# Input projections of a hybrid encoder in one core: pairs of units as seven block products, tokens in three parts

## Chip, core and metric

The kernel runs on one core of a Trainium2 chip. The core has a matmul engine (TensorE, PE), a vector engine (VectorE, DVE), an activation engine (ScalarE, ACT), a general engine (GpSimd, POOL) and a queue engine (SyncE, SP) that issues nearly all transfers; sixteen DMA engines move the data. The metric is the device time of one execution in microseconds (us), the median of several runs.

## What is computed

One step of an encoder layer with two attention branches, over 2,176 tokens (2,048 of a prompt, 128 of running streams) of width 1,024. Cut to the part that the change touches:

```
h    = rms_norm(x, g_in)                        # (2176, 1024)
proj = einsum('btd,de->bte', h, w_in)           # w_in: 1024 x 4928
qa, ka, va, z_a, qd, ckv_in, kpe_in, z_b, m_a, m_b = split(proj)
qa, ka = rope(qa, pos), rope(ka, pos)           # 512 columns each
# va: 512; z_a, z_b: 512 each, used as silu(z); qd: 512; ckv_in: 256; kpe_in: 64
# m_a, m_b: 1024 each, merge gates
```

Then come the latent projections, differential and latent attention, the gates, the output projections, the residual and a last normalisation. Everything is float32 outside. Inside, each factor of a large product is split into a rounded high part and a remainder (`hi`, `lo`, type float32r), and a product is three matmuls: hi x hi, hi x lo, lo x hi (`_mm3`, L94 to L101).

## The kernel before

`build` runs `_phase_a` (the input projections but for the merge gates), `_phase_a2` (latent projections), `_phase_b` (attention of the prompt), `_gates` (merge gates, groups of tokens that fill holes of the other stages), `_sample` (running streams) and `_phase_c` (output). Instructions are ordered by a list scheduler that simulates the engines: among those that are ready it takes the one with the highest priority, which is the program's order, except where code asks for another (`ahead()` in `_gates` asks for the priority that follows `_phase_a`). Tiles come from pools with a fixed number of buffers; a tile waits until the readers of the buffer's last tile are done.

In `_phase_a` the tokens stand transposed (`xT`, features on partitions), in six groups `GROUPS` of 384 columns (the last 256). `load_group` keeps the high and low parts of all groups in SBUF (`hi0` to `hi5`, `lo0` to `lo5`), scaled by the gain `g_in` but not by the tokens' root mean square. Squares are summed by GpSimd and VectorE, `stats` adds them over partitions with small matmuls and spreads 1/rms over R; R multiplies the results as they leave PSUM (L232, L233, L254, L260).

A unit is 128 columns of `w_in` (8 blocks of 128 features). For each group it takes 8 x 3 = 24 matmuls into one PSUM bank (`unit_psum`). 22 units are taken here: 4 for `qd`, 2 for `ckv_in`, 8 for rotary queries and keys (pairs, `rope_block`), 8 for the gates z (L260 to L263). `first_units` takes the first two as the groups arrive. Values run with tokens as the stationary operand, two passes of 256 columns (`v_block`); the rotary key of the latent branch has 16 matmuls a group (`kpe_block`). Between blocks, 16 further units for the merge gates are split and written to DRAM (`wz`), to be read by `_gates`.

Staging tiles for raw weights and tokens come from `c.zs` (2 buffers) and a pool of 1; split weights from `c.zw` (4) and a pool of 2; results from a pool of 6 and `c.zt` (4). `c.zh` holds group 0's tokens here, and later the tokens of `_gates`. Each split is a ScalarE copy (L112) and a VectorE subtraction (L113).

Of the kernel before, what the change touches and what calls it, by code (L numbers as in the profile page):

```python
# [38 lines left out]


# [4 lines left out]
def _consts(c, pool):  # L45
# [14 lines left out]
    c.rstd = pool.tile([P, NT], F32, name="rstd")  # L60
# [66 lines left out]
def _phase_a(c):  # L127
    nc, tc = c.nc, c.tc
    with (
        tc.tile_pool(name="a_h", bufs=1) as ph,  # L130
        tc.tile_pool(name="a_w", bufs=2) as pw,
        tc.tile_pool(name="a_s", bufs=1) as pst,
        tc.tile_pool(name="a_t", bufs=6) as pt,
# [3 lines left out]
        hi, lo, sums = [], [], []  # L137
        R = pc.tile([P, T], F32, name="R")
        count = {"st": 0, "w": 0, "t": 0}

        def stage(shape, name):
            count["st"] += 1
            return (pst if count["st"] % 3 == 0 else c.zs).tile(shape, F32, tag="st", name=name)

        def tmp(n, name, m=P):
            return pt.tile([P, NG], F32, tag="t", name=name)[:m, :n]

        def tmp2(n, name, m=P):
            return c.zt.tile([P, NG], F32, tag="t", name=name)[:m, :n]

        def load_group(g):
            t0, n = GROUPS[g]
            pool = c.zh if g < 1 else ph
            a = pool.tile([P, KT, n], F32R, tag=f"hi{g}", name=f"hi{g}")
            b = pool.tile([P, KT, n], F32R, tag=f"lo{g}", name=f"lo{g}")
            hi.append(a)
            lo.append(b)
            for k2 in range(4):
                if k2 % 2:
                    st = pc.tile([P, 2, NG], F32, tag="cs", name=f"xt{g}_{k2}", bufs=2)  # L160
                else:
                    st = stage([P, 2, NG], f"xt{g}_{k2}")
                nc.sync.dma_start(st[:, :, :n], c.i["xT"][:, 2 * k2 : 2 * k2 + 2, t0 : t0 + n])
                for k in range(2):
                    kt = 2 * k2 + k
                    gain = c.g_in[:, kt : kt + 1]
                    if k:
                        nc.gpsimd.tensor_scalar(a[:, kt, :], st[:, k, :n], gain, 1.0, op0=ALU.mult, op1=ALU.mult)
                    else:
                        nc.scalar.activation(a[:, kt, :], st[:, k, :n], AF.Copy, scale=gain)  # L170
                    nc.vector.scalar_tensor_tensor(
                        b[:, kt, :], st[:, k, :n], gain, a[:, kt, :].bitcast(F32), op0=ALU.mult, op1=ALU.subtract
                    )
                for k in range(2):
                    if k2 + k == 0:
                        total = pc.tile([P, NG], F32, tag="sq", name=f"sq{g}", bufs=2)[:, :n]
                        nc.scalar.square(total, st[:, k, :n])
                    else:
                        sq = tmp(n, f"sq{g}_{k2}_{k}")
                        nc.scalar.square(sq, st[:, k, :n])  # L180
                        (nc.gpsimd if k else nc.vector).tensor_tensor(total, total, sq, op=ALU.add)
            sums.append(total)

        def stats(g):
            t0, n = GROUPS[g]
            ta, tb = t0 // P, (t0 + n) // P
            ps = pp.tile([P, 512], F32, tag="ps", name=f"pss{g}")
            for t in range(tb - ta):
                nc.tensor.matmul(ps[:, t : t + 1], sums[g][:, t * P : (t + 1) * P], c.ones[:, 0:1], start=True, stop=True)
            nc.vector.tensor_copy(c.rstd[:, ta:tb], ps[:, : tb - ta])  # L190
            _rsqrt(c, c.rstd[:, ta:tb], c.rstd[:, ta:tb], 1.0 / D)
            yield
            ps = pp.tile([P, 512], F32, tag="ps", name=f"psr{g}")
            for t in range(ta, tb):
                dg = tmp(P, f"dg{t}")
                nc.vector.tensor_scalar(dg, c.ident, c.rstd[:, t : t + 1], None, op0=ALU.mult)
                nc.tensor.matmul(ps[:, (t - ta) * P : (t - ta + 1) * P], c.ones, dg, start=True, stop=True)
            nc.scalar.copy(R[:, t0 : t0 + n], ps[:, :n])
            nc.sync.dma_start(c.Rh[:, t0 : t0 + n], R[:, t0 : t0 + n])

        def weights(src, name):
            k, n = src.shape[1], src.shape[2]
            st = stage([P, k, n], f"ws_{name}")
            nc.sync.dma_start(st, src)
            count["w"] += 1
            pool = pw if count["w"] % 3 == 0 else c.zw
            a = pool.tile([P, k, n], F32R, tag="w", name=f"wh_{name}")
            b = pool.tile([P, k, n], F32R, tag="w", name=f"wl_{name}")
            _split(nc, a, b, st)
            return a, b  # L210

        def unit_psum(w, g, name, m=P):
            n = GROUPS[g][1]
            ps = pp.tile([P, 512], F32, tag="ps", name=f"ps_{name}_{g}")
            _mm3(
                nc, ps[:m, :n],
                [(w[0][:, kt, :], w[1][:, kt, :], hi[g][:, kt, :], lo[g][:, kt, :]) for kt in range(KT)],
            )
            return ps[:m, :n]

        def rope_block(u0, dst, pair, out, scale):
            ws = [weights(c.i["wu"][u0 + i], f"u{u0 + i}") for i in range(2)]
            for g, (t0, n) in enumerate(GROUPS):
                nm = f"r{u0}_{g}"
                pa = unit_psum(ws[0], g, f"u{u0}")
                pb = unit_psum(ws[1], g, f"u{u0 + 1}")
                cs = pc.tile([P, 2, NG], F32, tag="cs", name=f"cs{nm}", bufs=2)
                nc.sync.dma_start(cs[:, :, :n], c.i["rope"][:, :, t0 : t0 + n])
                co, si = cs[:, 0, :n], cs[:, 1, :n]
                Rg = R[:, t0 : t0 + n]  # L230
                ta, tb = tmp(n, f"ta{nm}"), tmp(n, f"tb{nm}")
                nc.vector.tensor_tensor(ta, pa, Rg, op=ALU.mult)  # L232
                nc.vector.tensor_tensor(tb, pb, Rg, op=ALU.mult)  # L233
# [7 lines left out]
                for half, (r, x, y) in enumerate(((m1, ta, m2), (m3, tb, m4))):  # L241
                    if out is not None:
                        nc.sync.dma_start(out[pair, half, :, t0 : t0 + n], r)
                    xr, yr = x.bitcast(F32R), y.bitcast(F32R)
                    nc.scalar.mul(xr, r, scale)
                    nc.vector.scalar_tensor_tensor(yr, r, scale, x, op0=ALU.mult, op1=ALU.subtract)
                    for hl, z in enumerate((x, y)):
                        nc.sync.dma_start(dst[pair, hl, half, :, t0 : t0 + n], z)
# [16 lines left out]
        def units(us):  # L265
            ws = [weights(src, nm) for src, nm, _ in us]
            for g in range(len(GROUPS)):
                for w, (src, nm, ev) in zip(ws, us):
                    ev(unit_psum(w, g, nm), g)
# [1116 lines left out]
```

## Time and profile before

| | |
|---|---|
| median of 3 runs | 2661.29 us (2658.8 to 2663.44) |
| profiled execution, its time | 2662.93 us |
| profiled execution, its span | 2661.1 us, 44,909 instructions |
| PE busy | 2513.8 us, 94% |
| DVE busy | 1442.7 us, 54% |
| ACT busy | 1066.6 us, 40% |
| POOL busy | 704.2 us, 26% |
| DMA | 496.17 MB, mean 186 GB/s |

Busy time is a union: two matmuls in flight count once, so the durations of single matmuls add up to more. The page also shows the granted clock of TensorE in tenths of 2.4 GHz; a timeline row gives the start, the duration, the engine, the line of the kernel, the operation with its output and inputs, and in brackets how long the engine sat idle before it and what ended that.

### The profile page before, as it was taken

What the parts mean: (1) busy time and instruction counts of PE and PEld (TensorE: products, weight loads), DVE (VectorE), ACT (ScalarE), POOL (GpSimd) and SP (SyncE); (2) the same over time, 40 slices, a digit from 0 to 9 for tenths busy, and PEclk for the clock granted to TensorE, in tenths of its full rate; (3) what the DMA queues carried; (4) which work ended last, traced back from release to release, by engine and by line L of the source; (5) the groups of instructions that cost most, each with busy time, mean ns of one, the idle gap of its engine ahead of it and who ended that gap; (6) DMA issues with size and microseconds to landing.
All of it is one profiled execution on the core that took longest, in us unless ns stands there. A gap on an engine that the chain in (4) does not pass through costs nothing. (4 is left out here: it accounts for less than half of the span.)

```text
span 2661.1 us, 44909 instructions
## 1 busy us (share of the span) xinstructions
PE 2513.8 (94%) x16308; PEld 2254.8 (85%) x16308; DVE 1442.7 (54%) x3038; ACT 1066.6 (40%) x2682; POOL 704.2 (26%) x946
## 2 busy tenths in 40 slices
PE   7999999999897989999999999998999997999998
PEld 7999899999787879998988898887676774888887
DVE  8236662233565657877785577896333323433333
ACT  5101213212333356766675566775334333311111
POOL 7102220001333333334343333544101001122221
PEclk9999999999898999999999999999999998999999
DMA  5346777422667893365566657523887676534332
GB/s 182 120 150 200 253 255 234 143 69 83 183 228 228 259 280 108 123 179 157 171 183 200 210 175 230 155 77 125 342 326 302 253 299 212 179 125 131 127 112 93
DMA packets 291372, 496.17 MB, mean 186 GB/s; under 512 B 27440, under 2 KB 229200, under 8 KB 280144
## 3 DMA queue, kind: packets, MB, share of 16 engines
q1 hardware_dynamic: 291152, 493.31, 56.3%
q8 instruction: 129, 2.11, 0.3%
q14 instruction: 91, 0.75, 0.1%
HBM read 351.55 MB, written 141.66 MB: 185 GB/s over the span
## 5 line engine op out<-in xcount | busy, mean ns | idle before, releaser
L98 PE MATMUL z<-z_hi,zw 128*128 128x384 f32 (+1 forms) x768 | 263.2, 343 | 26.2 <-ACT zt L388 22.1
L100 PE MATMUL z<-z_hi,zw 128*128 128x384 f32 (+1 forms) x768 | 257.2, 335 | 2.3 <-DMA zw<-wz 2.3
L99 PE MATMUL z<-z_lo,zw 128*128 128x384 f32 (+1 forms) x768 | 258.0, 336 | 0.6 <-POOL z_lo L370 0.6
L990 DVE TENSOR_REDUCE pmd<-sd 128x1 f32<-128x512 f32 (+3 forms) x320 | 189.4, 603 | 55.6 <-PE sd L1091 27.8
L992 ACT ACTIVATE ed<-sd,pmd 128x512 f32<-128x512 f32 (+3 forms) x320 | 200.4, 630 | 46.6 <-DVE pmd L990 32.8
L1091 PE MATMUL sd<-k,q 128*128 128x512 f32 (+2 forms) x640 | 189.9, 384 | 2.6 <-ACT ed L992 1.5
L1031 POOL TENSOR_SCALAR ed<-ed,ad 128x512 f32<-128x512 f32 (+3 forms) x160 | 116.2, 741 | 282.4 <-DVE ad L1007 129.3
L98 PEld LDWEIGHTS z<-z_hi,zw 128*128 128x128 f32 x768 | 148.2, 193 | 45.5 <-ACT zt L388 28.2
L99 PEld LDWEIGHTS z<-z_lo,zw 128*128 128x128 f32 x768 | 148.2, 193 | 8.9 <-issue 6.3
L100 PEld LDWEIGHTS z<-z_hi,zw 128*128 128x128 f32 x768 | 147.8, 192 | 8.2 <-issue 3.7
L1031 POOL TENSOR_SCALAR em<-em,am 128x512 f32<-128x512 f32 (+3 forms) x160 | 104.0, 665 | 152.3 <-DVE am L1007 93.0
L113 DVE TENSOR_TENSOR zw<-zs,zw 128x512 fp32r<-128x512 f32 x128 | 91.0, 737 | 86.2 <-ACT zw L112 85.9
L370 POOL TENSOR_TENSOR z_lo<-zx,z_hi 128x384 fp32r<-128x384 f32 (+1 forms) x48 | 48.3, 1032 | 333.0 <-DVE gt L260 262.7
L98 PE MATMUL y<-o,wh_ab 128*128 128x384 f32 (+1 forms) x384 | 127.8, 333 | 8.5 <-DVE sm L1212 8.5
L98 PE MATMUL ps_u<-hi,wh_u 128*128 128x384 f32 (+1 forms) x384 | 126.6, 330 | 7.5 <-ACT wh_u L112 7.5
L100 PE MATMUL y<-o,wl_ab 128*128 128x384 f32 (+1 forms) x384 | 126.7, 330 | 0.6 <-DVE wl_ab L113 0.6
L99 PE MATMUL y<-o,wh_ab 128*128 128x384 f32 (+1 forms) x384 | 126.8, 330 | 0.0
L99 PE MATMUL ps_u<-lo,wh_u 128*128 128x384 f32 (+1 forms) x384 | 126.2, 329 | 0.0
L98 PE MATMUL ps_z<-hi,wh_z 128*128 128x384 f32 (+1 forms) x384 | 125.2, 326 | 1.0 <-ACT wh_z L112 1.0
L100 PE MATMUL ps_u<-hi,wl_u 128*128 128x384 f32 (+1 forms) x384 | 125.3, 328 | 0.0
L99 PE MATMUL ps_z<-lo,wh_z 128*128 128x384 f32 (+1 forms) x384 | 125.1, 326 | 0.0
L100 PE MATMUL ps_z<-hi,wl_z 128*128 128x384 f32 (+1 forms) x384 | 124.9, 326 | 0.0
(364 smaller groups left out, 7436.6 us busy)
## 6 DMA issues: line engine op xcount, KB each, us to landing
zs<-in_wu_dram SPq DMA_DIRECT2D x64, 512.0 KB
zw<-wz SPq DMA_DIRECT2D x64, 512.0 KB
ksd<-in_ckT_dram SPq DMA_DIRECT2D x32, 1024.0 KB
vsd<-in_cv_dram SPq DMA_DIRECT2D x32, 1024.0 KB
q<-Qs SPq DMA_DIRECT2D x128, 128.0 KB
ksm<-in_cc_dram SPq DMA_DIRECT2D x16, 1024.0 KB
smT<-zt SPq DMA_DIRECT2D x80, 192.0 KB
sm<-smT SPq DMA_DIRECT2D x80, 192.0 KB
```

Of the source, the lines that this page charges most:

```text
L98: nc.tensor.matmul(out, ah, bh, start=(j == 0), stop=False)
L99: nc.tensor.matmul(out, ah, bl, start=False, stop=False)
L100: last = nc.tensor.matmul(out, al, bh, start=False, stop=(j == n - 1))
L113: nc.vector.tensor_tensor(lo, src, hi.bitcast(F32), op=ALU.subtract)
L370: nc.gpsimd.tensor_tensor(lo[:, k], x[:, j], hi[:, k].bitcast(F32), op=ALU.subtract)
L990: nc.vector.tensor_reduce(nm_, ps[:, :w], axis=AX.X, op=ALU.max, negate=True)
L992: nc.scalar.activation(e[:, :w], ps[:, :w], AF.Exp, bias=nm_, accum_out=l[:, s, i : i + 1])
L1031: nc.gpsimd.tensor_scalar(p, p, a[:, 0, j : j + 1], 1.0, op0=ALU.mult, op1=ALU.mult)
L1091: nc.tensor.matmul(ps[:, :n], qs[s][:, j, qc], ks[s].tiles[i][:, :n], start=(j == 0), stop=(j == 1 and not last))
```

## The change

The tokens are taken in three parts `PARTS` of 768, 768 and 640. For each part `stats` reads the untransposed tokens (`xn`), squares and sums each row on ScalarE, and spreads 1/rms over R. `load_part` then reads the transposed tokens, multiplies by gain and R, and splits them into X. X[0] holds the first four blocks of features, X[1] the other four, each for both halves of the part (`one`, `two`). Results need no further scaling.

A pair of units and a part make a product of 2 x 2 blocks: two units by two halves of the features, times two halves of the features by two halves of the tokens. It is computed with seven block products of 4 x 3 matmuls each (before: 8 x 3 matmuls for each unit and group). `sums` forms four differences of token blocks, in S, once per part; `pair_weights` forms four sums of weight blocks on GpSimd and splits seven operands; `pair_products` combines the seven results on VectorE. Weights are read and split once per part.

Values take all 512 columns at a time: `v_block` holds one PSUM bank for each of the part's six (five) groups of 128 tokens, feature block by feature block. The kept units are taken one after each of the first eight pairs of the first two parts. The next part's `stats` stands in the program after the ninth of eleven pairs; the pairs come as three latent ones, then rotary and gate pairs in turn. Staging has now 2 + 2 buffers, split weights 7 + 4, results 12 + 4; X, S and R have one buffer each. `c.rstd` is gone, and the layout of `wv` follows.

The diff, cut to the new functions (the removed ones stand in the code above; the rotary arithmetic, the stores and the outputs are as before where left out):

```diff
+PARTS = [(0, 384), (768, 384), (1536, 320)]
...
+        X = [
+            [(c.zh if i == 0 else ph).tile([P, 4, 2 * NG], F32R, tag=f"{l}{i}", name=f"x{l}{i}") for l in ("hi", "lo")]
+            for i in range(2)
+        ]
+        S = [[ph.tile([P, 4, NG], F32R, name=f"t{l}{i}") for l in ("h", "l")] for i in range(4)]
+        R = pc.tile([P, 2 * NG], F32, name="R")
+
+        def stats(p):
+            t0, n = PARTS[p]
+            nt = 2 * n // P
+            ss = pc.tile([P, 8], F32, tag="ss", name=f"ss{p}")[:, :nt]
+            for t in range(nt):
+                x = stage([P, D], f"xn{p}_{t}")
+                nc.sync.dma_start(x, c.i["xn"][t0 + t * P : t0 + (t + 1) * P, :])
+                nc.scalar.activation(x, x, AF.Square, accum_out=ss[:, t : t + 1])
+            r = pc.tile([P, 8], F32, tag="rs", name=f"rs{p}")[:, :nt]
+            _rsqrt(c, r, ss, 1.0 / D)
+            for a in range(0, nt, 3):
...
+                for t in range(a, min(a + 3, nt)):
+                    dg = tmp(P, f"dg{p}_{t}")
+                    nc.vector.tensor_scalar(dg, c.ident, r[:, t : t + 1], None, op0=ALU.mult)
+                    nc.tensor.matmul(ps[:, (t - a) * P : (t - a + 1) * P], c.ones, dg, start=True, stop=True)
+                nc.scalar.copy(R[:, a * P : a * P + w], ps[:, :w])
+            nc.sync.dma_start(c.Rh[:, t0 : t0 + 2 * n], R[:, : 2 * n])
+
+        def load_part(p):
...
+            for j in range(4):
+                for i in range(2):
+                    kt = j + 4 * i
+                    for half in range(2):
+                        cut = slice(half * n, half * n + n)
+                        x = tmp(n, f"x{p}_{kt}_{half}")
+                        nc.sync.dma_start(x, c.i["xT"][:, kt, t0 + half * n : t0 + half * n + n])
+                        nc.vector.scalar_tensor_tensor(x, x, c.g_in[:, kt : kt + 1], R[:, cut], op0=ALU.mult, op1=ALU.mult)
+                        hi, lo = (z[:, j, cut] for z in X[i])
+                        nc.scalar.copy(hi, x)
+                        nc.gpsimd.tensor_tensor(lo, x, hi.bitcast(F32), op=ALU.subtract)
+                        raw[j, i, half] = x
+            return raw
+
+        def sums(p, raw):
...
+                for i, out, x, y in ((0, b11, b12, b11), (2, b12, b22, b12), (1, b22, b22, b11), (3, b21, b21, b22)):
+                    nc.vector.tensor_tensor(out, x, y, op=ALU.subtract)
+                    hi, lo = (z[:, j, :n] for z in S[i])
+                    nc.scalar.copy(hi, out)
+                    (nc.gpsimd if i == 2 else nc.vector).tensor_tensor(lo, out, hi.bitcast(F32), op=ALU.subtract)
+
+        def v_block(p):
...
+            ps = [bank(f"psv{p}_{t}") for t in range(nt)]
+            for j in range(4):
+                st = stage([P, 2, 512], f"wsv{p}_{j}")
+                nc.sync.dma_start(st, c.i["wv"][j])
+                for i in range(2):
+                    w = operand([P, 2, 512], f"wv{p}_{j}_{i}")
+                    _split(nc, w[:, 0], w[:, 1], st[:, i])
+                    for t in range(nt):
+                        xh, xl = (z[:, j, t * P : (t + 1) * P] for z in X[i])
+                        first, last = j + i == 0, j == 3 and i == 1
+                        nc.tensor.matmul(ps[t], xh, w[:, 0], start=first, stop=False)
+                        nc.tensor.matmul(ps[t], xh, w[:, 1], start=False, stop=False)
+                        nc.tensor.matmul(ps[t], xl, w[:, 0], start=False, stop=last)
...
+        def pair_weights(u, nm, scale):
+            st = []
+            for i in range(2):
+                st.append(stage([P, KT, P], f"ws_{nm}_{i}"))
+                nc.sync.dma_start(st[i], c.i["wu"][u + i])
+            a11, a12, a21, a22 = (x[:, k : k + 4] for x in st for k in (0, 4))
+            s1, s2, s3, s4 = (pq.tile([P, 4, P], F32, tag=f"s{i}", name=f"s{i}_{nm}") for i in range(1, 5))
+            for out, x, y, op in (
+                (s1, a21, a22, ALU.add), (s2, s1, a11, ALU.subtract), (s4, a12, s2, ALU.subtract), (s3, a11, a21, ALU.subtract)
+            ):
+                nc.gpsimd.tensor_tensor(out, x, y, op=op)
+            ops = []
+            for i, x in enumerate((a11, a12, s4, s2, s3, s1, a22)):
+                w = operand([P, KT, P], f"w{i}_{nm}")
+                hi, lo = w[:, 0:4], w[:, 4:8]
+                nc.scalar.mul(hi, x, scale)
+                nc.vector.scalar_tensor_tensor(lo, x, scale, hi.bitcast(F32), op0=ALU.mult, op1=ALU.subtract)
+                ops.append(w)
+            return ops
+
+        def product(nm, w, z, cut):
+            ps = bank(nm)[:, : cut.stop - cut.start]
+            for k in range(4):
+                hi, lo = (x[:, k, cut] for x in z)
+                nc.tensor.matmul(ps, w[:, k], hi, start=(k == 0), stop=False)
+                nc.tensor.matmul(ps, w[:, k], lo, start=False, stop=False)
+                nc.tensor.matmul(ps, w[:, 4 + k], hi, start=False, stop=(k == 3))
+            return ps
+
+        def pair_products(p, u, nm, scale=1.0):
...
+            p1 = product(f"p1{nm}", a11, X[0], one)
+            nc.scalar.copy(m1, p1)
+            p2 = product(f"p2{nm}", a12, X[1], one)
+            p3 = product(f"p3{nm}", s4, X[1], two)
+            p6 = product(f"p6{nm}", s2, S[1], one)
+            add(v, p6, m1)
+            add(m1, p2, m1)
+            p7 = product(f"p7{nm}", s3, S[2], one)
+            add(u3, p7, v)
+            p5 = product(f"p5{nm}", s1, S[0], one)
+            add(v, p5, v)
+            add(w, p5, u3)
+            add(v, p3, v)
+            p4 = product(f"p4{nm}", a22, S[3], one)
+            add(u3, p4, u3)
+            return (m1, v), (u3, w)
...
+        def keep(u):
+            st = stage([P, KT, P], f"ws_z{u}")
+            nc.sync.dma_start(st, c.i["wu"][22 + u])
+            z = [operand([P, KT, P], f"w{l}_z{u}") for l in "hl"]
+            _split(nc, *z, st)
+            for l in range(2):
+                nc.sync.dma_start(c.wz[u, l], z[l].bitcast(F32))
...
+        spare = iter(range(16))
+        stats(0)
+        for p in range(len(PARTS)):
+            raw = load_part(p)
+            sums(p, raw)
+            v_block(p)
+            kpe_block(p)
+            for i, f in enumerate(pairs(p)):
                 f()
...
+                if i == 8 and p + 1 < len(PARTS):
+                    stats(p + 1)
+                if p < 2 and i < 8:
+                    keep(next(spare))
```

## Rows read from the trace of the kernel before

**Rows 1.** Busy time by stretch: length, engines, granted clock, DMA share, GB/s.
```profile
core 0: us, PE busy (x) PEld busy (x) DVE busy (x) ACT busy (x) POOL busy (x), PEclk, DMA share, GB/s
0.00:42.00 42.00, 25.94 (x121) 24.53 (x122) 34.75 (x45) 23.08 (x44) 29.45 (x40) 0.95 0.59 176
280.00:330.00 50.00, 44.53 (x270) 44.32 (x269) 32.50 (x49) 10.71 (x17) 11.12 (x10) 0.98 0.75 250
687.00:760.00 73.00, 59.96 (x312) 57.75 (x312) 49.27 (x69) 31.79 (x56) 31.52 (x27) 0.88 0.74 227
0.00:687.00 687.00, 657.25 (x4150) 654.13 (x4151) 318.47 (x505) 162.87 (x295) 120.05 (x128) 0.99 0.51 166
```
**Rows 2.** The gate units' bank: count, duration min/median/max, first and last start.
```profile
L98 PE MATMUL ps_z<-hi,wh_z x384: 278/334/441, 497.3 to 686.5; 128*128 128x384 f32 x160, 128*128 128x256 f32 x32
L100 PE MATMUL ps_z<-hi,wl_z x384: 280/334/337, 498.1 to 686.7; 128*128 128x384 f32 x160, 128*128 128x256 f32 x32
```
**Rows 3.** Timeline of TensorE, runs of matmuls of 256 and of 512 columns.
```profile
430.01 0.28 PE L99 MATMUL psv<-wl_v,hi 128*128 128x256 f32 x1
...
433.97 0.28 PE L99 MATMUL psv<-wl_v,hi 128*128 128x256 f32 x1
...
2299.80 0.40 PE L1226 MATMUL out<-wl_o,m 128*128 128x512 f32 x1
...
2302.07 0.39 PE L1227 MATMUL out<-wh_o,m 128*128 128x512 f32 x1
```
**Rows 4.** Timeline of TensorE at the start.
```profile
8.62 1.01 PE L98 MATMUL ps_qd<-hi,wh_qd 128*128 128x384 f32 x2 [8.62 <-ACT hi L170]
...
12.37 0.53 PE L100 MATMUL ps_qd<-hi,wl_qd 128*128 128x384 f32 x1
12.69 0.53 PE L98 MATMUL ps_qd<-hi,wh_qd 128*128 128x384 f32 x1
...
16.53 0.53 PE L98 MATMUL ps_qd<-hi,wh_qd 128*128 128x384 f32 x1
```
**Rows 5.** Timeline of ScalarE at the start: the first two units' weights.
```profile
5.53 1.04 ACT L112 CAST wh_qd<-ws_qd 128x1024 fp32r<-128x1024 f32 x1 [3.53 <-DMA ws_qd<-in_wu_dram]
6.83 1.04 ACT L112 CAST wh_qd<-ws_qd 128x1024 fp32r<-128x1024 f32 x1 [0.26 <-DMA ws_qd<-in_wu_dram]
```
**Rows 6.** Timeline of VectorE in a rotary block.
```profile
252.31 0.55 DVE L232 TENSOR_TENSOR tar<-ps_u,R 128x384 f32<-128x384 f32 x1
252.77 0.55 DVE L233 TENSOR_TENSOR tbr<-ps_u,R 128x384 f32<-128x384 f32 x1
255.65 1.02 DVE L236 TENSOR_TENSOR m1r<-tbr,csr 128x384 f32<-128x384 f32 x1 [2.33 <-DMA Qs<-tbr]
256.60 1.37 DVE L238 TENSOR_TENSOR m3r<-tar,csr 128x384 f32<-128x384 f32 x1
257.89 0.55 DVE L239 TENSOR_TENSOR m0r<-m0r,m1r 128x384 f32<-128x384 f32 x1
258.36 0.55 DVE L240 TENSOR_TENSOR m2r<-m2r,m3r 128x384 f32<-128x384 f32 x1
```
**Rows 7.** Timeline of GpSimd in the same stretch.
```profile
255.25 1.01 POOL L235 TENSOR_TENSOR m0r<-tar,csr 128x384 f32<-128x384 f32 x1 [5.42 <-DMA Qs<-m1r]
256.22 1.33 POOL L237 TENSOR_TENSOR m2r<-tbr,csr 128x384 f32<-128x384 f32 x1
```
**Rows 8.** Timeline of VectorE: two weight remainders of 512 elements, merged.
```profile
692.17 1.29 DVE L113 TENSOR_TENSOR zw<-zs,zw 128x512 fp32r<-128x512 f32 x2
```
**Rows 9.** Groups of GpSimd by line and shape: its two-input sums of 512 elements.
```profile
L1036 POOL TENSOR_TENSOR ed<-ed,ed 128x512 f32<-128x512 f32 x28 | 37.8, 1349 | 1.3 <-ACT ed L1035 1.2
```
**Rows 10.** Timeline of VectorE: tokens and first weights of the gates.
```profile
642.72 1.15 DVE L368 SCALAR_TENSOR_TENSOR zx<-zx,vec,Rz 128x384 f32<-128x384 f32 x2 [1.71 <-DMA zx<-in_xT_dram]
...
664.19 0.68 DVE L113 TENSOR_TENSOR zw<-zs,zw 128x512 fp32r<-128x512 f32 x1
```
**Rows 11.** Timeline of TensorE: the first matmul of the gates.
```profile
686.82 0.34 PE L98 MATMUL z<-z_hi,zw 128*128 128x384 f32 x1
```

More of the change, by code (lines that the diff above doesn't have):

```diff
@@ L145, in tmp, with operand @@
+        def operand(shape, name):
+            return turn("w", 3, pw, c.zw).tile(shape, F32R, tag="w", name=name)
         def tmp(n, name, m=P):
[L146 to L233, printed above, removed]
+            return turn("t", 4, pt, c.zt).tile([P, NG], F32, tag="t", name=name)[:m, :n]
@@ new lines, in product, with add @@
+        def product(nm, w, z, cut):
[7 more added lines that the diff above has]
+        def pair_products(p, u, nm, scale=1.0):
+            n = PARTS[p][1]
+            a11, a12, s4, s2, s3, s1, a22 = pair_weights(u, nm, scale)
+            one, two = slice(0, n), slice(n, 2 * n)
+            m1, v, u3, w = (tmp(n, f"{x}{nm}") for x in ("m1", "v", "u3", "w"))
+            def add(out, x, y):
+                nc.vector.tensor_tensor(out, x, y, op=ALU.add)
+            p1 = product(f"p1{nm}", a11, X[0], one)
[14 more added lines that the diff above has]
+            return (m1, v), (u3, w)
@@ new lines, in rope_pair @@
+        def rope_pair(p, u, dst, pair, out, scale):
+            t0, n = PARTS[p]
+            res = pair_products(p, u, f"r{u}_{p}")
+            for half in range(2):
+                nm = f"r{u}_{p}_{half}"
+                cols = slice(t0 + half * n, t0 + half * n + n)
+                cs = pc.tile([P, 2, NG], F32, tag="cs", name=f"cs{nm}", bufs=2)[:, :, :n]
+                nc.sync.dma_start(cs, c.i["rope"][:, :, cols])
+                co, si = cs[:, 0], cs[:, 1]
+                ta, tb = res[0][half], res[1][half]
@@ L265, in units @@
[L265 to L269, printed above, removed]
-        def first_units(us):
-            ws = [weights(src, nm) for src, nm, _ in us]
-            todo = []
-            for g in range(len(GROUPS)):
-                load_group(g)
-                ps = [unit_psum(w, g, u[1]) for w, u in zip(ws, us)]
-                for f in todo:
-                    f()
-                st = stats(g)
-                next(st)
-                todo = [lambda st=st: next(st, None)]
-                todo += [lambda p=p, ev=u[2], g=g: ev(p, g) for p, u in zip(ps, us)]
-            for f in todo:
-                f()
@@ L337, in _phase_a @@
[L337 to L347 removed]
+                        nc.sync.dma_start(dst[pair, hl, a, :, cols], z)
```

159 lines of the change are left out of this document (76 added, 83 removed).

## Prediction

> **What bounds the kernel now.** I read the page first for the span and the busy tenths, then the busy times by stage, then single instructions on the timelines. The first projections (`_phase_a`) end where the last `ps_z` matmul starts, at 686.7 us of 2661.1 [rows 1, 2]. In that stretch TensorE is busy 657 of 687 us at a granted clock of 0.99, VectorE 318, ScalarE 163, GpSimd 120, and the DMA share is 0.51 at 166 GB/s. The reader is to see that only TensorE is full there. So the stage is worth what its matmuls are worth, until one of the changes fills another engine.
>
> A "busy" matmul overlaps the next one, so I take the spacing of starts. The 1,152 `ps_z` matmuls start within 189.4 us: 0.1645 us each [rows 2]. One in six has 256 columns, and 256 columns are spaced 0.120 us (33 steps from 430.01 to 433.97) [rows 3], so 384 columns take (6 x 0.1645 - 0.120)/5 = 0.173 us. 512 columns take 0.227 us (ten steps from 2299.80 to 2302.07) [rows 3]. 320 columns appear nowhere; midway between 256 and 384 is 0.1465 us, with 0.120 and 0.173 as bounds.
>
> The stage before, in spacings: 22 units x 24 x 6 = 3,168 matmuls x 0.1645 = 521 us; values 816 x 0.120 = 98; rotary key 96 x 0.1645 = 16; the small sums of `stats` some 8. That is 643 of 687 us. The other 44 are the start (first matmul at 8.62 us), waits of the first block for its tokens (in the first 42 us TensorE is busy 26) and stretches at the lower clock after waits [rows 1, 4].
>
> **The change part by part.** *Products.* Each pair of units and part takes seven products of 12 matmuls: 84 instead of 2 x 24 per group of tokens. Two parts with 384 columns: 2 x 11 x 84 x 0.173 = 320 us. The third: 11 x 84 x 0.1465 = 135 us (bounds 111 and 160). Together 455 against 521, a gain of 66.
>
> *Values.* 17 x 24 = 408 matmuls of 512 columns x 0.227 = 93 us against 98: 5 less. The rotary key stays at 16. Squares and sums move from TensorE, GpSimd and VectorE to ScalarE's accumulated Square, and 17 small matmuls that spread R remain, about 2 us against 8. TensorE's work after: 455 + 93 + 16 + 2 = 566 us, 77 less.
>
> *Start.* The first matmul now needs R, so six 512 KB tiles of `xn`, a square each, the root, the spread over R, then the first token tile. The second 512 KB of weights was usable 1.30 us after the first, which was usable at 5.53 [rows 5]; at that pace six tiles are in at 12 us. At the 176 GB/s of the first 42 us [rows 1] it is 3.1 MB/176 = 18 us after the first landing, some 21. Behind that come about 4 us of root, diagonal, matmul and copies. First matmul between 15 and 32; I take 25, as four staging buffers for six tiles put it nearer the slow pace. After it each 4 us of value matmuls needs two token tiles, 2 x 1.01 us of GpSimd [rows 7]: covered. TensorE comes out of idleness at the low clock: from 12.37 to 16.53 the matmuls are spaced 0.32 us instead of 0.173 [rows 4]. That is 2 to 3 us at each such start; 4 in all.
>
> *Part boundaries.* X and S have one buffer. The next part's tokens can be written as the last pair's p1, p2 and p3 finish; p6, p7, p5 and p4 then still run 48 x 0.173 = 8 us, which hides the first tiles. Sixteen temporaries hold a whole part's tokens, and the last pair holds eight of them until its outputs have left, so the second half of the tokens comes late, behind 16 us of value matmuls. What is late next is VectorE: about 44 operations of 384 columns (tokens, differences) and the value splits, some 30 us, plus GpSimd's share, under 38 us of value and key matmuls. I take 6 us for each of two boundaries; bounds 0 and 20.
>
> *Weights, sums and rotary work on VectorE.* This is the term that decides. An operation of 384 columns is spaced 0.46 to 0.47 us there when GpSimd is still (252.31 to 252.77, 257.89 to 258.36), one of 512 columns 0.60 (two in 1.29 us, the second ending 0.69 after it starts) [rows 6, 8]. Take a rotary pair with the gate pair behind it: TensorE 168 x 0.173 = 29.1 us. VectorE: 14 weight remainders x 0.60 = 8.4; 14 sums out of PSUM x 0.47 = 6.6; rotary 12 x 0.47 = 5.6; gates 4 x 0.47 = 1.9: 22.5 us, and five of eight pairs of the first two parts also split a kept unit (1.1 us each, twice a 512 one). GpSimd: eight sums of weights of 512 elements x 1.35 us [rows 9] and four rotary products x 1.01 [rows 7]: 14.8 us.
>
> The two engines disturb each other. VectorE's products at 255.65 and 256.60 take 2.24 us to the next start instead of 0.94, while GpSimd's two run from 255.25 to 257.55 [rows 6, 7]: VectorE loses 1.3 us to 2.3 us of GpSimd, 0.56 per us. If that holds for all of GpSimd's time, VectorE needs 22.5 + 8.3 = 30.8 us; if only while it works on operands that both lie in SBUF (15.9 of its 22.5), 28.3. Two kept units add 2.3. So VectorE stands at 28 to 33 against TensorE's 29.1. The two engines wait for each other in order, so I charge 2 us to each of the 12 such couples, 24 us; bounds 0 (VectorE fits) and 8 each (below). For the three latent pairs of a part VectorE has about 11 us under 14.5: covered. ScalarE has some 8 us of casts and copies under 14.5: covered; without that cover it would cost nothing until it doubled.
>
> The far end is that the two never run at once on such operands. The four instructions would take 2.96 us one after another and took 2.72 (255.25 to 257.97, the last one's end), so they overlap little [rows 6, 7]. Without any overlap the couple needs 22.5 + 14.8 = 37.3 us, or 30.7 where all 6.6 us of PSUM sums fall into GpSimd's time.
>
> The Trainium skill (SBUF — State Buffer, Who interferes with whom) has this as a rule: an operation of VectorE with two SBUF inputs and one of GpSimd that reads SBUF exclude each other for whole instructions, whichever starts first. The trace agrees nearly, with its 2.72 of 2.96 us [rows 6, 7], and by the rule the couple lies at that far end and the change would lose; by the loss of 0.56 per us it wins.
>
> *DMA.* Weights are read three times (35 MB instead of 12, kept units apart), `wv` three times, and `xn` once more: some 37 MB on top of 114 MB. At 151 MB in about 630 us it is 240 GB/s. A couple with two kept units moves 8.4 MB in 29.1 us, 288 GB/s. In the rotary block 250 GB/s came with a share of 0.75, so about 330 if full [rows 1]. I price it at nothing; TensorE's 29.1 us is the cover, and if it moved only 250 GB/s each such couple would cost 4.5 us more.
>
> *Hand-over.* Before, the tokens of the first gate group are normalised during the last block (zx from 642.72) and the gate matmuls begin at 686.82 as the stage ends [rows 10, 11]. Now their tiles are X[0], which is read until p1 of the last pair, 14 us before the end. Tokens and the first weights took from 642.72 to 664.88, with waits [rows 10]; I expect two gate units (2 x 24 x 0.173 = 8 us) to slip. TensorE is idle 13 of the 73 us behind [rows 1], but other gates fill such holes as well. I take 8; bounds 0 and 17.
>
> **Sum.** The stage: 566 + 25 + 4 + 12 + 24 = 631 us against 687: 56 less. With the hand-over 48 less. The profiled execution took 2662.9 us for its span of 2661.1, 1.6 above the median of the runs shown: 2614.9, or 2613 on the scale of the median. I say 2614.
>
> **Rivals.** *Shared operands make VectorE and GpSimd the bound.* If they never overlap, at 37.3 us a couple, it costs 8 us for each of 12 couples, 96 instead of 24, and some 15 more are lost at the heads of the three parts (20 us of GpSimd a part at 0.56 is 11, of which I had counted half under cover): 2614 + 72 + 15 = 2701, slower. It decides from some 6 us a couple (24 + 48 = 72/12). For it: the four instructions above [rows 6, 7]. Against it: 6.6 us of PSUM sums that can run during GpSimd's time, and VectorE's waits for stores there, which show slack [rows 6]. Chance 0.13.
>
> *Tokens late at the heads of the parts.* Start at 32 and boundaries at 20 each: 7 + 28 = 35 more, 2649. For it: single buffers, sixteen temporaries. Against: the value block needs few tiles at a time. 0.14.
>
> *DMA is the bound in the couples with kept units.* 4.5 us for five of eight couples, and 8 for the heads: some 35 to 45 more, 2655. Against it: 250 GB/s came with a share of 0.75. 0.05.
>
> *All hidden.* VectorE fits and the hand-over is free: 2614 - 24 - 8 = 2582. 0.08.
>
> **Chances.** The forecast has 0.60. 0.2% (5.3 us) is about what a measurement of this kernel tells from no change. Faster by more: the forecast, the hidden case and most of the late tokens, 0.79; same 0.07; slower 0.14. The range reaches from below the hidden case, 2578, to just above no change, 2668, and leaves the first rival out. The forecast's own range is 2590 to 2645.
>
> **What would show it.** In the changed kernel the stage should end between 610 and 655 us; the first value matmul should start near 25 us; products should be spaced 0.173 us for 384 columns, 0.147 for 320 and 0.227 for 512. VectorE should be busy in over 85% of the couples' stretches with TensorE at 85 to 100%. TensorE waiting there for weight remainders (L113's successor) or for free banks says VectorE is the bound; for a DMA, that the queue is. Wrong would be the forecast if TensorE's share of the couples fell under 0.8, if a boundary showed over 20 us of idle TensorE, or if the stages behind grew by more than 17 us.

## The result and the profile after

The changed kernel takes 2729.73 us (median of 4 runs, 2725.52 to 2738.30) against 2662.36 (4 runs of the kernel before): a ratio of 1.0258, 95% interval 1.0237 to 1.0279. It is slower by 67 us where I had forecast 48 us faster, and it lies above the range.

The page of the kernel after, its busy line:
```profile
PE 2459.8 (90%) x15470; PEld 2177.6 (80%) x15470; DVE 1722.7 (63%) x3422; ACT 1219.8 (45%) x3010; POOL 951.4 (35%) x1084
```
TensorE has 54 us less to do than before and the program takes 65 us longer in its span (2726.0). Its stretches, as in [rows 1]: the whole stage, a stretch of couples (a rotary pair of units with the gate pair behind it), a stretch around the head of the second part, and the 73 us behind the stage:
```profile
core 0: us, PE busy (x) PEld busy (x) DVE busy (x) ACT busy (x) POOL busy (x), PEclk, DMA share, GB/s
0.00:723.50 723.50, 598.83 (x3310) 576.05 (x3310) 586.76 (x873) 308.92 (x612) 361.91 (x262) 0.92 0.62 203
100.00:200.00 100.00, 85.36 (x473) 84.72 (x472) 80.12 (x115) 37.53 (x68) 52.42 (x36) 0.92 0.70 232
200.00:300.00 100.00, 74.25 (x384) 70.95 (x383) 82.98 (x123) 43.32 (x83) 43.03 (x33) 0.84 0.67 228
723.50:796.50 73.00, 37.79 (x162) 35.97 (x163) 44.08 (x58) 27.82 (x48) 27.47 (x21) 0.74 0.75 224
```
The reader is to see three things. The stage ends at 723.4 us instead of 686.7, though TensorE is busy 58 us less in it. VectorE went from 318 to 587 us and GpSimd from 120 to 362 [rows 1], and in the 100 us around the head of the second part TensorE is busy 74% at a granted clock of 0.84. Behind the stage TensorE is busy 38 of 73 us, against 60 [rows 1].

TensorE's main waits in the timeline of the kernel after (the bracket is the idle time and what ended it):
```profile
23.03 0.50 PE L227 MATMUL psv<-wv,xhi 128*128 128x512 f32 x1 [3.00 <-ACT xhi L198]
71.29 0.69 PE L259 MATMUL ps_kpe<-xhi,w_kpe 128*128 128x384 f32 x1 [10.90 <-ACT v L234]
159.77 0.69 PE L289 MATMUL p2r<-xhi,w_r 128*128 128x384 f32 x1 [8.54 <-DVE vg L302]
239.89 1.19 PE L182 MATMUL psr<-dg,ones 128*128 128x128 f32 x4 [13.50 <-DVE dg L181]
241.20 0.52 PE L290 MATMUL p1r<-xlo,w_r 128*128 128x384 f32 x1
242.80 0.52 PE L289 MATMUL p1r<-xhi,w_r 128*128 128x384 f32 x1
285.53 0.79 PE L227 MATMUL psv<-wv,xhi 128*128 128x512 f32 x1 [12.24 <-ACT xhi L198]
328.88 0.69 PE L259 MATMUL ps_kpe<-xhi,w_kpe 128*128 128x384 f32 x1 [5.47 <-ACT v L234]
495.20 1.19 PE L182 MATMUL psr<-dg,ones 128*128 128x128 f32 x4 [19.26 <-DVE dg L181]
535.36 0.79 PE L227 MATMUL psv<-wv,xhi 128*128 128x512 f32 x1 [8.20 <-ACT xhi L198]
575.92 0.63 PE L289 MATMUL p1l<-xhi,w_l 128*128 128x320 f32 x1 [6.53 <-ACT v L234]
738.98 0.69 PE L99 MATMUL z<-z_hi,zw 128*128 128x384 f32 x1 [15.60 <-ACT zw L113]
```
The heads of the second and third part hold most of it: the wait for 1/rms (`dg`), then for the first token (`xhi`), then for the value results to leave their banks. Waits for a sum out of PSUM (`vg`) are those of the couples. After each wait matmuls of 384 columns come every 0.32 us for a while (five steps from 241.20 to 242.80), as in [rows 4]: the lower of the two clock levels, 1.2 GHz.

VectorE at the head of the second part:
```profile
221.75 1.64 DVE L336 TENSOR_TENSOR m0r<-m0r,m1r 128x384 f32<-128x384 f32 x1
223.32 1.64 DVE L343 SCALAR_TENSOR_TENSOR m1r<-m0r,m1r 128x384 fp32r<-128x384 f32 x1
224.88 0.55 DVE L343 SCALAR_TENSOR_TENSOR m3r<-m2r,u3r 128x384 fp32r<-128x384 f32 x1
...
230.80 0.54 DVE L302 TENSOR_TENSOR u3g<-p7g,vg 128x384 f32<-128x384 f32 x1
231.26 1.15 DVE L362 SCALAR_TENSOR_TENSOR gs<-gs,m1g 128x384 f32<-128x384 f32 x1
...
233.73 0.27 DVE L181 TENSOR_SCALAR dg<-ident,rs 128x128 f32<-128x128 f32 x1
...
236.80 1.75 DVE L281 SCALAR_TENSOR_TENSOR w_g<-ws_g,w_g 128x512 fp32r<-128x512 f32 x1
238.47 3.08 DVE L181 TENSOR_SCALAR dg<-ident,rs 128x128 f32<-128x128 f32 x5
...
281.97 2.56 DVE L196 SCALAR_TENSOR_TENSOR x<-x,vec,R 128x384 f32<-128x384 f32 x3 [4.83 <-DMA x<-in_xT_dram]
```
and GpSimd in the same stretch:
```profile
221.51 1.47 POOL L275 TENSOR_TENSOR s_r<-ws_r 128x512 f32<-128x512 f32 x1
222.94 1.61 POOL L275 TENSOR_TENSOR s_r<-ws_r,ws_r 128x512 f32<-128x512 f32 x1
224.51 1.66 POOL L109 TENSOR_TENSOR rs<-ss,mhalf 128x6 f32<-128x6 f32 x1
...
230.28 1.72 POOL L275 TENSOR_TENSOR s_r<-ws_r,s_r 128x512 f32<-128x512 f32 x1
...
238.07 1.59 POOL L275 TENSOR_TENSOR s_g<-s_g,ws_g 128x512 f32<-128x512 f32 x1
...
278.02 1.26 POOL L275 TENSOR_TENSOR s_l<-ws_l 128x512 f32<-128x512 f32 x1 [14.46 <-DMA ws_l<-in_wu_dram]
```
An operation of VectorE on two SBUF tiles that starts while GpSimd forms a sum ends some 0.4 us after that sum: `m0r` at 221.75 takes 1.64 us (the sum at 221.51 ends at 222.98), `m1r` at 223.32 again 1.64. The sum out of PSUM at 230.80 takes 0.54, although GpSimd works from 230.28 to 232.00; `gs` at 231.26, from SBUF, takes 1.15. Roots are ready at 226.2 on GpSimd, but the first diagonal comes at 233.73 and the other five at 238.47, behind this backlog and a weight remainder of 1.75 us. Two of the five, which started during the sums at 238.07 and 239.74, took 1.28 and 1.29 us instead of 0.27, though a `dg` has one SBUF tile as its input. Not all of the head is backlog: before its first token operation, at 281.97, VectorE stood idle 4.83 us for the token's transfer.

Groups of VectorE and of GpSimd by shape, from 60 us to the end of the stage (count | busy us, mean ns | idle before):
```profile
L281 DVE SCALAR_TENSOR_TENSOR w_r<-ws_r,w_r 128x512 fp32r<-128x512 f32 x36 | 41.2, 1158 | 6.5 <-ACT w_r L280 6.5
L302 DVE TENSOR_TENSOR vr<-p6r,m1r 128x384 f32<-128x384 f32 x8 | 4.4, 552 | 1.3 <-PE p6r L291 1.3
L275 POOL TENSOR_TENSOR s_g<-ws_g 128x512 f32<-128x512 f32 x12 | 25.6, 2137 | 36.7 <-DMA ws_g<-in_wu_dram 21.9 <-DVE w_r L281 11.7 <-DMA ws_r<-in_wu_dram 3.1
L275 POOL TENSOR_TENSOR s_l<-s_l,ws_l 128x512 f32<-128x512 f32 x8 | 11.4, 1420 | 0.1
```
The remainder that took 0.68 us alone [rows 8, 10] takes 1.16 in the mean in rotary pairs, the sum of two weight blocks 1.35 to 2.14, by tile, where I had priced 1.35 [rows 9].

### The profile page after: what moved, and what is told of

It reads as the page before. It is cut to its first block, busy times and chain, and to the rows that moved or that the text cites. A ratio compares the mean times of both kernels' runs of the same rounds, so it can differ in the third digit from the quotient of the medians.

```text
span 2726.0 us, 44441 instructions
## 1 busy us (share of the span) xinstructions
PE 2459.8 (90%) x15470; PEld 2177.6 (80%) x15470; DVE 1722.7 (63%) x3422; ACT 1219.8 (45%) x3010; POOL 951.4 (35%) x1084
## 5 line engine op out<-in xcount | busy, mean ns | idle before, releaser
L1261 POOL TENSOR_TENSOR sm<-sm,sm 128x384 f32<-128x384 f32 (+1 forms) x48 | 48.2, 1004 | 264.3 <-DVE sm L1258 264.3
L1038 ACT ACTIVATE em<-sm,pmm 128x512 f32<-128x512 f32 (+3 forms) x160 | 100.2, 628 | 66.2 <-DVE pmm L1036 57.7
L1036 DVE TENSOR_REDUCE pmm<-sm 128x1 f32<-128x512 f32 (+3 forms) x160 | 96.0, 603 | 46.4 <-PE sm L1180 30.2
L1095 DVE TENSOR_TENSOR ptld<-ptd,pthd 128x512 fp32r<-128x512 f32 (+3 forms) x160 | 96.0, 603 | 45.3 <-ACT pthd L1094 44.4
L1258 DVE SCALAR_TENSOR_TENSOR sm<-sm,y 128x384 f32<-128x384 f32 (+1 forms) x96 | 50.2, 529 | 114.8 <-PE y L101 114.8
L1094 ACT CAST pthd<-ptd 128x512 fp32r<-128x512 f32 (+3 forms) x160 | 83.1, 523 | 83.2 <-PE ptd L1091 82.4
L1095 DVE TENSOR_TENSOR ptlm<-ptm,pthm 128x512 fp32r<-128x512 f32 (+3 forms) x160 | 95.9, 602 | 32.1 <-ACT pthm L1094 31.0
```

The lines of the kernel that those rows point to most:

```text
L1036: nc.vector.tensor_reduce(nm_, ps[:, :w], axis=AX.X, op=ALU.max, negate=True)
L1038: nc.scalar.activation(e[:, :w], ps[:, :w], AF.Exp, bias=nm_, accum_out=l[:, s, i : i + 1])
L1094: nc.scalar.copy(hi, v)
L1095: nc.vector.tensor_tensor(ptl[ch][:, :n, i * P : (i + 1) * P], v, hi.bitcast(F32), op=ALU.subtract)
```

## Experiments

Each kernel was timed against the kernel before on the same chip; ratios are to that. The end of the stage and TensorE's wait behind it are read from the timeline of the one profiled execution: the start of the first matmul that is not of the stage, less its idle time (in the kernel before, the start of the stage's last matmul).

| kernel | ratio (95% interval) | stage ends, us | span behind it |
|---|---|---|---|
| before | 1 | 686.7 | 1974.4 |
| after: seven products, sums on GpSimd | 1.0258 (1.0237 to 1.0279) | 723.4 | 2002.6 |
| 1. eight products | 1.0007 (0.9990 to 1.0023) | 675.7 | 1987.9 |
| 2. seven, no sums of weights | 1.0003 (0.9986 to 1.0021) | 649.1 | 2006.6 |
| 3. seven, 1/rms earlier | 1.0142 (1.0113 to 1.0170) | 687.9 | 2003.4 |
| 4. before, last block backwards | 1.0080 (1.0049 to 1.0111) | 684.1 | 1990.9 |
| 5. as 3, own token tiles | 1.0119 (1.0100 to 1.0138) | 695.4 | 2000.0 |
| 6. seven, sums on VectorE | 1.0075 (1.0050 to 1.0100) | 689.2 | 1995.9 |
| 7. as 2, 1/rms earlier | 0.9932 (0.9910 to 0.9955) | 642.1 | 2010.6 |
| 8. eight, own tiles | 0.9995 (0.9983 to 1.0007) | 673.1 | 1989.0 |
| 9. as 6, 1/rms earlier | 1.0078 (1.0057 to 1.0098) | 680.0 | 1993.0 |
| 10. as 1, 1/rms earlier | 1.0067 (1.0054 to 1.0080) | 676.0 | 1995.7 |
| 11. as 10, own tile for X[0] | 1.0029 (1.0016 to 1.0041) | 676.4 | 1981.4 |

**1. Eight products.** The parts, the early normalisation, the values and the order stay; each unit takes 24 matmuls for each half of a part, from four split operands a pair, without sums, differences or S; ScalarE copies the results.

```diff
+                for k in (0, 4):
+                    x = st[:, k : k + 4]
...
+            for i in range(2):
+                for half in range(2):
...
+                    for kt in range(KT):
+                        a, k = ops[2 * i + kt // 4], kt % 4
+                        hi, lo = (x[:, k, cut] for x in X[kt // 4])
...
+                    nc.scalar.copy(t, ps)
```


> The three parts, the normalised tokens and the 512-column values stay, but a pair of units takes eight products again: four split operands instead of seven, no sums of weights, no differences of tokens, four copies on ScalarE in place of seven sums on VectorE. Theory A (the heads of the parts, where TensorE stood idle 10.9 + 31.2 + 34.0 us, and the hand-over to the gates hold the loss): TensorE's products grow by 66 us, the couples' 27 us of waits and some 10 of the heads go, so about 2730 + 66 - 37 = 2759 us. Theory B (VectorE and GpSimd are the bound everywhere, and the waits at the heads are their backlog): with VectorE relieved the stage is TensorE's 632 us and a start of 23, some 665, so about 2730 - 58 = 2672 us.

Measured 2660.59 against 2656.24 us. The three parts and the wide values alone cost nothing and bring nothing; the seven products cost 2.5%, some 67 us, against eight in the same frame. The stage's row:
```profile
0.00:675.70 675.70, 640.92 (x3706) 621.92 (x3706) 308.80 (x466) 276.02 (x564) 119.23 (x116) 0.99 0.65 220
```

**2. No sums of weights.** GpSimd's four sums of each pair are left out.

```diff
-                nc.gpsimd.tensor_tensor(out, x, y, op=op)
...
-            for i, x in enumerate((a11, a12, s4, s2, s3, s1, a22)):
+            for i, x in enumerate((a11, a12, a12, a21, a11, a22, a22)):
```


> The four sums of weight blocks on GpSimd are left out (132 instructions, some 210 us busy of GpSimd); the split operands are raw blocks instead, so the results differ, and all else stays. Theory A: the couples' waits of 27 us shrink and the heads' stay: 2700 to 2715 us. Theory B: VectorE gets back 0.56 us for each us of GpSimd, some 110 us of the stage, and the heads shrink with its backlog: 2640 to 2670 us.

Measured 2656.90 us: all of the loss is gone, about 68 us on this chip's scale, for 132 instructions of GpSimd (11 pairs, 3 parts, 4 sums). The stage's row:
```profile
0.00:649.20 649.20, 582.74 (x3310) 561.51 (x3310) 519.58 (x872) 311.93 (x612) 158.90 (x130) 0.97 0.67 226
```
VectorE runs as many instructions as after and is busy 67 us less: that is what 203 us less of GpSimd gives back. By the two stage rows its idle time hardly changes (129.6 us, 136.7 after), so 67 of the 74 us by which the stage is shorter lie in VectorE's busy time. The waits of the couples (over 3 us) are gone; those at the heads (8.9 and 8.6 us for 1/rms, 12.0 and 9.1 for tokens) and behind the stage (15.6) stay. Against experiment 1 the stage ends 27 us earlier, and the program 4 us.

**3. 1/rms of the next part after the third pair instead of the ninth.**

```diff
-                if i == 8 and p + 1 < len(PARTS):
+                if i == 2 and p + 1 < len(PARTS):
```


> The next part's sums of squares and R stand after the third pair of a part instead of after the ninth. Theory A: TensorE's two waits for the diagonals of R (13.5 and 19.3 us) go and nothing takes their place, with 2 us each for the clock: about 2730 - 37 = 2693 us. Theory B: VectorE's work is the same and the waits come back as others: 2722 to 2735 us.

Measured 2693.43 us, some 31 us less than the changed kernel by the ratios. The waits for 1/rms:
```profile
128.22 1.65 PE L182 MATMUL psr<-dg,ones 128*128 128x128 f32 x6 [4.89 <-DVE dg L181]
268.18 0.80 PE L227 MATMUL psv<-wv,xhi 128*128 128x512 f32 x1 [13.54 <-ACT xhi L198]
```
The first fell from 13.5 to 4.9 us, the second from 19.3 to under 2; the waits for tokens are as long as they were. The gain is near theory A's 37 us.

**4. The kernel before, its last block of gate units over the groups backwards**, so that group 0's tile is read to the end, as X[0] is not quite in the changed kernel.

```diff
-            for g in range(len(GROUPS)):
+            order = range(len(GROUPS))
+            for g in reversed(order) if us[-1][1] == "z7" else order:
```


> The kernel before, with one change: its last block of two gate units takes the token groups from last to first, so the tile of group 0, which the gates' first tokens need, is read until the end of the stage, as X[0] is after the change. If the hand-over costs what the two traces suggest (28 us of the 65 us of longer span lie behind the stage): 2678 to 2690 us. If the gates only slip into later holes: 2657 to 2668 us, and the 28 us come from something else.

Measured 2677.15 us, 21 more. The amount of work is the same, only its order differs, and with it when tiles come free; behind the stage TensorE then waits 17 us:
```profile
701.39 1.44 PE L446 MATMUL pss<-ones,sq 128*128 128x1 f32 x6 [17.26 <-DVE sq L438]
```
So this order costs 21 us, more than the bound of 17 that I had set. That all of it is the late tile of group 0 is not shown: the order also changes when the other groups' tiles come free.

**5. As 3, with five buffers of their own for the first token tiles of a part.**

```diff
+        tc.tile_pool(name="a_x", bufs=5) as px,
...
+                        if 4 * j + 2 * i + half < 5:
+                            x = px.tile([P, NG], F32, tag="x", name=f"x{p}_{kt}_{half}")[:, :n]
```


> As e3_stats_early (2693 us), and the first five token tiles of a part have buffers of their own instead of sharing the sixteen temporaries with the last pair's results. In e3 TensorE stood 13.5 and 9.8 us at the heads of the second and third part for the first tokens. If the temporaries hold the tokens back, most of that goes, with some 4 us for the clock: 2670 us. If the tokens wait for their place in the transfer queue or for VectorE's backlog: 2688 to 2698 us.

Measured 2696.78 against 2664.19 us: 0.2% under the third experiment, within the intervals. The wait for tokens fell from 13.5 to 2.4 us at the second part and went at the third, but the waits for 1/rms (7.7 and 5.3 us, 4.9 and under 2 in the third experiment) and for the banks of the values (12.1 us at the first part and 8.1 at the second, 9.6 and under 1 there) grew in its place. The temporaries were late, but not what limits.

**6. The sums of weights on VectorE**, which then has 132 instructions more.

```diff
-                nc.gpsimd.tensor_tensor(out, x, y, op=op)
+                nc.vector.tensor_tensor(out, x, y, op=op)
```


> The changed kernel with its four sums of weight blocks a pair on VectorE instead of GpSimd. If VectorE's own load is the bound, 132 sums x 0.60 us are added and the time rises to some 2729 + 79 = 2800 us. If the two engines exclude each other on operands in SBUF, the sums cost VectorE 79 us but give back the 0.56 us for each of GpSimd's 210 us (118), and the chain of four sums gets shorter: 2690 us.

Measured 2685.05 against 2664.19 us: 1.8% less than with GpSimd's help. The stage's row and the group of remainders:
```profile
0.00:689.30 689.30, 594.02 (x3310) 567.16 (x3310) 595.92 (x1001) 310.47 (x611) 171.90 (x130) 0.96 0.65 213
```
```profile
L281 DVE SCALAR_TENSOR_TENSOR w_r<-ws_r,w_r 128x512 fp32r<-128x512 f32 x36 | 27.4, 772 | 1.5 <-ACT w_r L280 1.5
```
VectorE does 128 more instructions in the stretch and is busy 9 us longer (595.9 against 586.8); GpSimd is busy 190 us less. The remainders fell from 1158 to 772 ns. This tells sharing apart from load: if VectorE had only been full, more work on it would have cost time.

It does not tell sharing apart from a shorter chain of sums. By the stage's rows VectorE's idle time fell from 136.7 to 93.4 us, which is more than the stage got shorter. In the kernel after, VectorE stood idle 95 us for ScalarE's copies of weight operands (`w_l`, `w_r` and `w_g`, L280), here 40; and ScalarE stood idle 108 us for GpSimd's sums. The largest of these waits in the kernel after (us in total, times, longest):
```profile
DVE w_l L281 <- ACT w_l L280: 40.8, 19, 7.1
ACT w_r L280 <- POOL s_r L275: 51.7, 9, 9.3
```
In the mean by tile a sum takes 0.68 to 0.83 us on VectorE here and took 1.35 to 2.14 on GpSimd. How much of this experiment's gain is the shorter chain, no run isolates.

**7. As 2, with 1/rms early: both edits at once, so again without the sums.**

> Both e2 and e3: no sums of weight blocks (raw blocks are split in their place, the results differ) and the next part's R after the third pair. Alone they gave 73 and 37 us. If R's waits were a cost of their own, the two add up: about 2662 - 40 = 2622 us on the scale of the median before. If R was late mostly because VectorE waited behind GpSimd's sums, little is left to gain beyond e2's two waits of 9 us: 2640 to 2650 us.

Measured 2646.20 us, ratio 0.9932: 0.7% under the second experiment, against 1.2% that the same edit gave with the sums. By the two ratios the place in the program was worth some 19 us without the sums, against 31 with them; with intervals of several us each, the difference, which would be VectorE's backlog behind GpSimd, is not sure. This is also the most that seven products showed with their sums for nothing: 18 us.

**8. Eight products; X[0] and all sixteen token tiles in buffers of their own.**

```diff
+        tc.tile_pool(name="a_x", bufs=16) as px,
...
-            [(c.zh if i == 0 else ph).tile([P, 4, 2 * NG], F32R, tag=f"{l}{i}", name=f"x{l}{i}") for l in ("hi", "lo")]
+            [ph.tile([P, 4, 2 * NG], F32R, tag=f"{l}{i}", name=f"x{l}{i}") for l in ("hi", "lo")]
...
-                        x = tmp(n, f"x{p}_{kt}_{half}")
+                        x = px.tile([P, NG], F32, tag="x", name=f"x{p}_{kt}_{half}")[:, :n]
```


> Eight products as in e1, and the room that S and the sums leave is used: X[0] no longer lies in the tile that the gates' first tokens need, and all sixteen token tiles of a part have buffers of their own. In e1 TensorE stood 7.8 and 7.1 us at the heads of the parts and 17.7 us behind the stage. If the hand-over and the temporaries cause these: 2660 - 13 - 17 = 2630 us, ahead of both kernels. If the gates only slip into later holes: 2645 us; if neither helps: 2660 us.

Measured 2664.31 us, ratio 0.9995. The waits at the heads and behind the stage went, but waits of 5.8 and 8.1 us came within the first 40 us, and the first latent product (`qn`) starts at 732.8 us, as in the first experiment (732.2). No gain: a miss.

**9. Sums on VectorE and 1/rms early: the edits of 6 and 3.**

> Seven products, the sums of weights on VectorE instead of GpSimd, and the next part's stats after the third pair instead of the ninth. Theory A (sums on GpSimd and the late 1/rms are two costs; a part of the second is VectorE's backlog behind GpSimd, so that only the half that remained without sums, 18 us, is added): from a ratio of 1.0075 with the sums on VectorE to about 1.0005, 2660 to 2670 us. Theory B (the two are fully additive, 37 us): 0.994. Theory C (VectorE with 132 more operations is itself the bound, and work for the heads taken earlier only pushes the couples back): 1.005 or more.

Measured 2676.33 against 2654.92 us, ratio 1.0078: as the sixth, so theory C. The head of the second part:
```profile
240.00:266.00 26.00, 10.78 (x63) 10.46 (x61) 24.12 (x41) 8.73 (x17) 6.25 (x5) 0.77 0.86 296
```
```profile
266.11 0.80 PE L227 MATMUL psv<-wv,xhi 128*128 128x512 f32 x1 [15.33 <-ACT xhi L198]
```
VectorE is busy 24 of 26 us there and TensorE 11: freed from the wait for 1/rms, the head waits for VectorE's own work, in which the next pair's four sums of weights (258.57 to 262.13) stand ahead of the tokens.

**10. Eight products and 1/rms early: the edits of 1 and 3.**

> Eight products, three parts, and the next part's stats after the third pair. Without sums of weights the two waits for 1/rms are 7.8 and 7.1 us at the heads of the parts. Theory A (these waits are lost time): they go, and with the slow clock after them some 15 to 18 us, ratio about 0.994. Theory B (as with the token tiles of their own, the wait comes back elsewhere in the part): 0.998 to 1.002.

Measured 2672.22 us, ratio 1.0067: slower by 0.6% than the first, which neither theory said. The premise was wrong, since the two waits there are for tokens, not for 1/rms, and the edit leaves them as they were:
```profile
255.24 0.79 PE L225 MATMUL psv<-wv,xhi 128*128 128x512 f32 x1 [7.61 <-ACT xhi L196]
```
The stage ends at 676.0 as before the edit (675.7), yet the latent products start at 743.5 instead of 732.2. Where the 11 us come from in that stretch was not found.

**11. As 10, with X[0] in its own tiles (the second line of 8).**

> As the last, and X[0] in its own tiles instead of the tile that the merge gates use next, so that the gates' tokens can be loaded before the last product has read X[0]. Theory A (the wait of 17.7 us for the gates' tokens at the end of the stage is the cost of the shared tile, and time lost): the wait goes and the ratio falls by a further 0.004 to 0.006. Theory B (the start of the latent projections, whose weights come one after the other, sets the end of this stretch, and the gates only fill it): within 0.0015 of the last.

Measured 2664.22 us, ratio 1.0029, 0.4% under the tenth: at the edge of theory A. The gates begin at 676.4 us, and the wait of 19.2 us behind the stage became this one and others of at most 7.2:
```profile
690.16 0.69 PE L99 MATMUL z<-z_hi,zw 128*128 128x384 f32 x1 [3.49 <-ACT zt L408]
```

No version beat the kernel before by more than the measurement tells, but for the seventh, which leaves sums out.

## Why the prediction was wrong

**What held.** TensorE's spacings and the work that followed from them; the first value matmul at 23.0 us (25 predicted); the couples' own waits, 28 us in all (24); the rotary key's and values' blocks but for their banks; and DMA as a rate (203 GB/s in the stage, while 296 came in a stretch of experiment 9), though single transfers were waited for.

**The step that failed first: the loss between VectorE and GpSimd, charged to the couples alone.** I took 2 us for each of 12 couples. Experiment 2 prices GpSimd's sums at about 68 us. TensorE's idle waits in the couples are only 28 us of the changed kernel; the rest is at the heads, where VectorE arrives with a backlog and then waits for the first tokens (4.8 and 3.2 us), and in the slow clock after each wait. The first rival, shared operands, is what decided: it named the mechanism and 2701 us, and I gave it 0.13. Its size was wrong in another way. In the stage 203 us of GpSimd (361.9 - 158.9) cost VectorE 67 us, 0.33 us per us, less than the 0.56 of [rows 6, 7]; the couples did not need 37.3 us each. But each delay is passed on to what stands behind it in VectorE's queue, as the rows of `dg` above show. A second path was not in the sum either: VectorE waits for ScalarE's copies, and those for GpSimd's chain of sums (95 and 108 us above); its share of the loss was not isolated.

The Trainium skill (SBUF — State Buffer, Who interferes with whom) says which operations share: those of VectorE with two SBUF inputs, and of those with at most one only the ones in its two-port modes. The trace agrees on the first: 552 ns for the sums out of PSUM, 1.64 us beside 0.55 for the others. The `dg`, with one SBUF tile, took 1.28 us beside 0.27; whether they ran in such a mode no row shows. The prediction used the rule only for the far end of the couple.

**The part boundaries: 6 us each predicted, 31 and 34 measured** (13.5 + 12.2 + 5.5 and 19.3 + 8.2 + 6.5), above my bound of 20. I had looked at the tokens' tiles and at the engine's total in that stretch, and not at `stats`: placed after the ninth pair, its diagonals stand in VectorE's queue behind everything of the last couples. Experiment 3 gives 31 us for this place alone; 7 against 2 gives some 19 without the sums; 9 shows the head limited by VectorE afterwards (24 of 26 us). Experiment 5 rules out the temporaries as the limit.

**The slow clock: 4 us predicted.** TensorE is busy 598.8 us in the stage where the spacings give 566, 33 more, at a granted clock of 0.92; before it was 657 against 643 at 0.99 [rows 1], so not all of the 33 is the clock. I had priced the start alone, and each of a dozen waits has its own. In experiment 2, with fewer waits, it is 583 us at 0.97: 16 of the 33 go.

**The hand-over: 8 us predicted, 28 measured** (2002.6 - 1974.4 us behind the stage). Experiment 4's order, which reads group 0's tile to the end, costs the kernel before 21 us, and 11 against 10 shows that X[0]'s place costs 0.4%; 8 against 1, with the token tiles changed as well, shows no gain beyond the intervals. But the time behind the stage also grows when the stage gets shorter: experiment 2 ends it 27 us before experiment 1 and is only 4 us faster. The latent products of these two start almost together, as the rows of the latent query weights show (first and last start; after, experiment 1, experiment 2):
```profile
L99 PE MATMUL qn<-qh,wh_uq x96: 277/334/667, 798.9 to 971.5; 128*128 128x384 f32 x80, 128*128 128x256 f32 x16
```
```profile
L99 PE MATMUL qn<-qh,wh_uq x96: 278/334/667, 732.2 to 906.1; 128*128 128x384 f32 x80, 128*128 128x256 f32 x16
```
```profile
L99 PE MATMUL qn<-qh,wh_uq x96: 277/334/668, 728.1 to 907.7; 128*128 128x384 f32 x80, 128*128 128x256 f32 x16
```
They start 75, 56 and 79 us behind the stage; in the kernel before it was 50 (the first at 736.8). Which of that stretch's loads, splits and gate units holds them was only looked at, not isolated; and experiment 10 shows 0.6% from a different order with the same stage. This part stays open.

**The sum of the miss** is 2729.7 - 2614 = 116 us: boundaries 53 (65 - 12), slow clock 29 (33 - 4), the wait of 10.9 for the first part's value banks, couples 4, start -2, hand-over 20. That is 115. It says where the time is lost, not by what. Of the other rivals, late tokens at the heads had the right place, but taking VectorE's wait for them away gained nothing (experiment 5); DMA as the bound and everything hidden are out.

## What to carry to other kernels

Fewer block products trade matmuls for elementwise work: here 58 us less of TensorE in the stage (640.9 to 582.7, experiments 1 and 2) cost 211 us more of VectorE (308.8 to 519.6) before one sum of weights was formed, and TensorE then waited for it. Before work goes to GpSimd to relieve VectorE, count which of VectorE's operations have two SBUF inputs: moving 132 sums back onto VectorE made this kernel 1.8% faster, by less sharing and a shorter chain together. And a step that sits at the end of a part and feeds the head of the next is priced by what is queued ahead of it on its engine, not by the engine's total.

## What the runs showed of the hardware

The loss goes both ways: a sum of 512 elements took GpSimd 1.26 us where VectorE was idle (278.02 to 281.80) and 1.35 to 2.14 in the mean, by tile, from 60 us to the end of the stage. VectorE's busy time was the same with 132 sums of weights on it as with the sums on GpSimd (1725.6 and 1722.7 us in the whole program). Operations of 384 columns with one input from PSUM took 0.54 to 0.56 us whatever GpSimd did. One SBUF input is not always safe: the `dg` took 1.28 and 1.29 us during GpSimd's sums and 0.27 to 0.28 outside them in the stage.
